# Negated blocks, the addition of value halves, swaps of maxima and a written order in a hybrid attention block

## The chip, the cores and the metric

The kernel runs on one core of one Trainium2 chip. The core has five engines that run their own instructions in order and wait for each other through semaphores: TensorE (PE, matrix products; PEld is its weight load), VectorE (DVE), ScalarE (ACT), GpSimd (POOL) and SyncE (SP, which here only issues transfers). ACT and POOL issue transfers too. The metric is the device time of one execution in microseconds, as the median of three runs. Lower is better.

## The reference

One decoder block in float32 on 1024 tokens, with 16 learned meta tokens ahead of them, a width of 1024 and 8 heads of 64. What matters of it:

```python
h = rmsnorm(x, norm_g)
u_pool, z_pool, q, k, v, z_attn, f, g_pool, g_attn = split(h @ w_in)
y_pool = causal_multiscale_pool(u_pool, pool_w, pool_scale) * silu(z_pool)
log_f = log_sigmoid(f + b_forget)
s = q @ k.T / sqrt(64) + c_query - c_key        # c = cumsum(log_f), causal
y_attn = (softmax(s) @ v) * silu(z_attn)        # per head
merged = sigmoid(g_pool) * (y_pool @ w_up_pool) + sigmoid(g_attn) * (y_attn @ w_up_attn)
out = rmsnorm(x + merged @ w_out, final_norm_g)  # the meta rows are dropped
```

## The kernel before

A float32 product is made of three products of a rounded type: each operand is split into a high and a low part, and hi·hi, hi·lo and lo·hi are summed in PSUM. So an operand always passes a split before PE can use it: the high part is a rounding copy (ACT), the low part a subtraction (POOL for weights, DVE or POOL for activations).

**Stages.** From 0 to about 88 us the input is normalised, transposed into `hh4` and `hl4` (high and low part of the activations, which stay in SBUF) and the queries, keys and values of the first pair of heads are made. From 88 to 520 us run the 16 `Unit`s of the attention: four pairs of heads, two heads each, two halves of the queries each. A unit of the first half has five blocks of keys, one of the second half nine. From 520 to 620 us PE makes the projections `z_pool` and `z_attn` with seven block products where a plain scheme has eight (`g_prod`, 0 to 6, L932), for which sums of blocks of the weights (`GS`) and of the activations (`HS`) are needed. Then come the pooling products, the up projections and the gates (to 707 us), and the output product in seven block products again, with sums of blocks of `w_out` (`TD`).

**The order in the attention.** PE's order is written out by hand. For each unit the scores of the next one (`a_steps`) and the softmax and value products of this one (`c_steps`) are merged, and between them the object `F` ("fill") draws in matmuls of the projections (L164): as many as PACE times the DVE time of a step leaves free, and fixed amounts, LM1 and LM2 (in ns of PE), around `maxes`. The other engines' order is made by a scheduler from the dependencies, and `after(x, y)` adds one by hand.

**Weights.** `split_w` (L141 to L152) loads 128 columns of the weights into a buffer with the tag `raw` (two buffers, SP, L145), and makes the high part on ACT (L150) and the low part on POOL (L152).

**Sums of blocks.** They are made in DRAM during the attention. `put` (L579) is a transfer that SP issues, `add` (L582) one that POOL issues and that adds to its target. The table `SUMS` says which of them follow which unit. `put_neg` (L590) makes the negative of a block of activations: it loads half of the block from DRAM into a tile `neg` with the tag `raw`, ACT negates it (L594) and SP stores it (L595). The tag is that of the weights, so `neg` takes turns with them in the same two buffers.

**Maxima.** `maxes` (L675) takes the running maximum of a unit's scores, transposes it (L678), reduces it (L680), and needs the maximum over four groups of 32 partitions, for which two small copies swap the halves (L682) and four swap the quarters (L685), with a `max` after each (L683, L686). All is on DVE.

**The end of a unit.** `finish` (L721): the value product `po` holds two halves that must be added. ACT copies 64 rows to the tile `t` (L725), DVE adds the others (L726), SP stores the sum to `sp_y` (L727). The row sums `acc` (made on POOL, L707 to L710) are transposed and reduced on DVE (L729, L731) and stored (L732).

**Behind the attention** the scheduler sets the order of ACT, DVE and POOL too. There `w_in_` and `h_in` load blocks of weights and activations, `w_split` (L912) and `h_split` (L921, L922 for product 2, whose activations are negated, and L924, L925 for the others) split them, `keep` (L941), `silu` (L944) and `plus_` (L947) take products out of PSUM, `pool_chain` (L862, L868) makes the moving sums of the pooling branch, `sums_in` (L884 to L889) the reciprocals of the row sums, and `attn_norm` (L841, L842) loads and applies these.

## Time and profile before

| | before |
|---|---|
| runs | 793.66, 793.96, 795.17 us |
| median | 793.96 us |
| the profiled execution's own time | 793.09 us |
| its span | 791.4 us |
| mean granted clock of TensorE | 0.968 |

The profile is one execution; its span runs from the first instruction to the last, and 1.7 us lie around it. In the windows view, each stage's busy time (us; its length; then busy us of each engine with the number of instructions; the granted clock of TensorE as a share of full speed; the busy share of the DMA engines, which can pass 1 where transfers queue; GB/s) reads:

```profile
0.00:88.00 88.00, 85.36 (x570) 74.71 (x571) 46.78 (x117) 49.92 (x110) 28.64 (x50) 1.00 0.32 95
520.00:620.40 100.40, 92.86 (x391) 74.97 (x390) 60.80 (x57) 51.05 (x68) 64.13 (x59) 0.95 0.61 195
707.50:791.40 83.90, 76.35 (x349) 63.52 (x347) 60.23 (x90) 40.71 (x88) 30.02 (x49) 0.98 0.25 89
```

A stage is full where PE's busy time is near its length. Names such as `pj`, `whi` or `neg` are those of the program's tiles; `a<-b` is an instruction that writes a and reads b; x16 is a count; `SPq L145` is the issue of a transfer, and `DMA` the transfer itself. Several figures with slashes are the shortest, median and longest duration.

### The profile page before, as it was taken

To read this page: it belongs to the slowest core of one execution; us is meant where nothing else is said; L and a number is where in the kernel's file an instruction comes from. 1 tells how busy PE (TensorE), PEld (TensorE's weight loads), DVE (VectorE), ACT (ScalarE), POOL (GpSimd) and SP (SyncE) were. 2 spreads that over 40 slices of the span, in tenths; PEclk is the share of its full clock that TensorE was granted. 3 is DMA by queue.
4 is the path that set the end of the run, shared out by engine and by line. 5 is a ranking of instruction groups with operands and counts; after the bars stand their busy time and mean duration, and the time that the engine had idled before them with its cause. 6 is when DMAs were issued, how large, how long until landed. Compare 5 with 4: busy or idle time off the path is not lost.

```text
span 791.4 us, 10759 instructions
## 1 busy us (share of the span) xinstructions
PE 730.7 (92%) x3637; PEld 620.7 (78%) x3637; DVE 554.0 (70%) x1023; ACT 398.3 (50%) x814; POOL 340.2 (43%) x404
## 2 busy tenths in 40 slices
...
PEclk9999999999599979999999999999799999999999
...
GB/s 299 41 28 46 45 83 192 253 33 184 263 35 15 212 263 98 231 91 180 198 64 212 216 179 187 62 276 315 216 147 16 224 107 234 257 241 133 0 1 213
DMA packets 91241, 120.44 MB, mean 152 GB/s; under 512 B 11041, under 2 KB 54049, under 8 KB 91058
## 3 DMA queue, kind: packets, MB, share of 16 engines
...
## 4 chain that ended last, share of the span: by engine, by line
PE 68%; DMA 9%; DVE 8%; ACT 5%; issue 3%; POOL 1%; SPq 0%; POOLq 0%; DVEq 0%; ACTq 0%
PE pj L164 41%; PE pj L1148 8%; PE pj L932 7%; PE po L718 3%; DMA raw<-in_w_in_dram 3%; PE pt L932 2%; PE pt L1148 2%; DMA hsn<-neg 2%; PE ps L657 2%; PE ps L658 2%; ACT S L666 1%; DVE pl L702 1%; DVE m L673 1%; DMA rc<-recs 1%; DMA sp_u<-st 1%
## 5 line engine op out<-in xcount | busy, mean ns | idle before, releaser
L164 PE MATMUL pj<-hh,whi 128*128 128x512 f32 (+3 forms) x640 | 149.1, 360 | 31.8 <-ACT whi L150 28.7
L164 PEld LDWEIGHTS pj<-hh,whi 128*128 128x128 f32 x640 | 110.2, 192 | 45.2 <-ACT whi L150 29.6
L164 PE MATMUL pj<-hl,whi 128*128 128x512 f32 (+3 forms) x640 | 145.5, 354 | 0.0
L152 POOL TENSOR_TENSOR wlo<-raw,whi 128x256 fp32r<-128x256 f32 x116 | 92.7, 886 | 119.3 <-ACT whi L150 61.7
L164 PE MATMUL pj<-hh,wlo 128*128 128x512 f32 (+3 forms) x640 | 143.0, 350 | 0.0
L164 PEld LDWEIGHTS pj<-hl,whi 128*128 128x128 f32 x640 | 109.8, 191 | 12.1
L164 PEld LDWEIGHTS pj<-hh,wlo 128*128 128x128 f32 x640 | 108.4, 188 | 11.9
L702 DVE TENSOR_TENSOR pl<-S,ph 128x512 fp32r<-128x512 f32 (+4 forms) x112 | 88.6, 806 | 15.5 <-ACT ph L701 14.9
L710 POOL TENSOR_TENSOR acc<-acc,S 128x272 f32<-128x272 f32 (+4 forms) x80 | 76.1, 952 | 13.6 <-ACT S L698 8.9
L666 ACT ACTIVATE S<-ps,negc 128x400 f32<-128x400 f32 (+2 forms) x96 | 49.1, 517 | 57.4 <-DVE S L664 54.9
L136 POOL TENSOR_TENSOR gw<-graw,gw 128x256 fp32r<-128x256 f32 x48 | 50.6, 1089 | 39.6 <-ACT gw L912 17.2
L673 DVE TENSOR_TENSOR m<-m,S 128x272 f32<-128x272 f32 (+4 forms) x80 | 48.0, 601 | 26.8 <-ACT S L666 25.3
L698 ACT ACTIVATE S<-S 128x512 f32<-128x512 f32 (+4 forms) x112 | 49.7, 479 | 31.4 <-DVE S L697 31.2
L150 ACT ACTIVATE whi<-raw 128x512 fp32r<-128x512 f32 x58 | 34.2, 623 | 41.0 <-DMA raw<-in_w_in_dram 28.9
L701 ACT ACTIVATE ph<-S 128x512 fp32r<-128x512 f32 (+4 forms) x112 | 51.9, 479 | 1.8 <-PE po L718 1.4
L932 PE MATMUL pj<-gh,gw 128*128 128x512 f32 x180 | 45.8, 411 | 7.5 <-ACT gh L921 6.1
L697 DVE TENSOR_TENSOR S<-S,pt 128x512 f32<-128x512 f32 (+4 forms) x112 | 51.5, 496 | 0.8
L932 PEld LDWEIGHTS pj<-gh,gw 128*128 128x128 f32 x180 | 35.6, 200 | 16.8 <-ACT gh L921 7.3
L657 PE MATMUL ps<-qa,ka 128*128 128x512 f32 (+4 forms) x112 | 38.8, 347 | 7.8 <-ACT S L666 7.3
L1040 DVE TENSOR_TENSOR rl<-pj,rl 128x512 f32<-128x512 f32 x32 | 22.1, 689 | 31.3 <-PE pj L164 31.3
L718 PE MATMUL po<-pl,V 128*128 128x512 f32 (+4 forms) x112 | 38.7, 345 | 3.6 <-DVE pl L702 3.4
L658 PE MATMUL ps<-ql,ka 128*128 128x512 f32 (+4 forms) x112 | 38.3, 342 | 0.0
...
## 6 DMA issues: line engine op xcount, KB each, us to landing
raw<-in_w_in_dram SPq DMA_DIRECT2D x31, 512.0 KB, 6.2
xt<-in_x_dram SPq DMA_DIRECT2D x8, 512.0 KB, 6.7
...
```

The source lines that it names most:

```text
L152: ins = nc.gpsimd.tensor_tensor(lo[:, k:k + 2], raw[:, k:k + 2], r32(hi[:, k:k + 2]), op=ALU.subtract)
L164: nc.tensor.matmul(ps, a, b, start=(i == 0), stop=(i == len(seq) - 1))
L657: nc.tensor.matmul(ps[:kb, c0:], ka[:, k0:k0 + kb], qa[:, q0 + c0:q0 + 512], start=True, stop=False)
L658: nc.tensor.matmul(ps[:kb, c0:], ka[:, k0:k0 + kb], ql[:, q0 + c0:q0 + 512], start=False, stop=True)
L666: nc.scalar.activation(s[:kb, f0:], ps[:kb, f0:], AF.Identity, bias=nb_)
L673: nc.vector.tensor_tensor(m[:kb, c0:], m[:kb, c0:], s[:kb, c0:], op=ALU.max)
L701: nc.scalar.activation(ph[:kb, c0:], s[:kb, c0:], AF.Copy)
L702: dves.append(nc.vector.tensor_tensor(pl[:kb, c0:], s[:kb, c0:], r32(ph[:kb, c0:]), op=ALU.subtract))
L710: accs.append(nc.gpsimd.tensor_tensor(acc[:kb, c0:], acc[:kb, c0:], s[:kb, c0:], op=ALU.add))
L718: nc.tensor.matmul(self.po[:, c0:], v, r[:kb, c0:], start=(b == 0 and i == 0), stop=(b == self.nb - 1 and i == 1))
L932: nc.tensor.matmul(ps, op_w[n][p][k // 2][:, k % 2, i * 128:(i + 1) * 128], op_h[n][q][k // 2][:, k % 2], start=start and m == 0, stop=m = ...
L1148: nc.tensor.matmul(ps, pick(A_, k, p)[:, i * 128:(i + 1) * 128], pick(B_, k, q)[:, c0:c1], start=start and n == 0, stop=n == 11, skip_grou ...
```

## The change

It has four parts.

1. *Negated blocks.* `put_neg` takes 128 rows at a time. It has a buffer of its own (`neg`, 128 x 512), is fed by the split activations that are in SBUF (ACT writes −hi, POOL subtracts the low part in two pieces of 256 columns) and stores the result straight to the places of the sums that need it (`HS` X and A, or C). The blocks 12, 21, n12 and n21 in DRAM are gone, the table of sums is written anew, with 14 adding transfers in place of 16, and the first copies of `TD` 1 and 3 stand next to each other behind unit 4.
2. *The end of a unit.* ACT copies all of `po` to `t`, SP stores one half, and an adding transfer of POOL brings the other half to the same place. DVE's addition is gone.
3. *Maxima.* The six small copies of `maxes` are on ACT.
4. *Order.* PACE goes from 1.74 to 1.67, LM2 from 2600 to 3200. Behind the attention the order of PE, ACT, DVE and POOL is written by hand: `h_split` makes both high parts first, the loads and sums stand earlier, and `attn_norm` later. `pool_chain` is a generator, so that it can be taken in steps. A few tiles have other buffers (`grow`, the weights of product 2), and a low part of the pooling branch moved from POOL to DVE.

```diff
@@ -31,10 +31,10 @@
-PACE = 1.74
+PACE = 1.67
-LM1, LM2 = 1400.0, 2600.0
+LM1, LM2 = 1400.0, 3200.0
...
@@ -397,7 +397,7 @@
-    grow = ap_.tile([1, D], F32, name="grow", tag="t")
+    grow = gp.tile([1, D], F32, name="grow", tag="g")
...
@@ -564,7 +564,7 @@
-    HS = {n: dr.tile([512, 512], F32, name=f"hs{n}") for n in ("11", "12", "21", "22", "n12", "n21", "A", "B", "C", "X")}
+    HS = {n: dr.tile([512, 512], F32, name=f"hs{n}") for n in ("11", "12", "21", "22", "A", "B", "C", "X")}
...
@@ -587,29 +587,41 @@
     def add_h(n):
         add(rows_of(HS[n]), hblock(hl4, n))
 
-    def put_neg(n):
-        for k in range(2):
-            t = wp.tile([128, 2, 512], F32, name="neg", tag="raw")
-            put(t, rows_of(HS[n])[:, 2 * k:2 * k + 2])
-            after(nc.scalar.activation(t, t, AF.Copy, scale=-1.0), exps[-1])
-            nc.sync.dma_start(rows_of(HS["n" + n])[:, 2 * k:2 * k + 2], t)
+    def put_neg(blk, k, *dsts):
+        t = ap_.tile([128, 512], F32, name="neg")
+        after(nc.scalar.activation(t, hblock(hh4, blk)[:, k], AF.Copy, scale=-1.0), exps[-1])
+        for c in range(0, 512, 256):
+            sub = nc.gpsimd.tensor_tensor(t[:, c:c + 256], t[:, c:c + 256], hblock(hl4, blk)[:, k, c:c + 256],
+                                          op=ALU.subtract)
+            after(sub, accs[-1])
+        for d in dsts:
+            put(HS[d][128 * k:128 * k + 128], t)
+
+    def n21(k):
+        put_neg("21", k, "X", "A")
+
+    def n12(k):
+        put_neg("12", k, "C")
+
+    def add_s(d, n):
+        add(rows_of(HS[d]), rows_of(HS[n]))
 
     SUMS = {
-        0: [(put_h, "21"), (put_h, "12")],
-        1: [(add_h, "21"), (put, GS[1], GB["11"])],
-        2: [(add_h, "12"), (put, GS[3], GB["12"])],
-        3: [(put_neg, "21"), (add, GS[1], GB["12"])],
-        4: [(put, TD[1], WB["11"]), (put, TD[3], WB["12"]), (add, GS[3], GB["22"])],
-        5: [(put_neg, "12"), (put_h, "11")],
-        6: [(add, TD[1], WB["12"]), (add_h, "11"), (put, GS[2], GS[3])],
-        7: [(add, TD[3], WB["22"]), (put_h, "22"), (put, HS["X"], HS["n21"])],
-        8: [(add_h, "22"), (add, rows_of(HS["X"]), rows_of(HS["11"]))],
-        9: [(put, TD[2], TD[3]), (put, HS["A"], HS["22"]), (add, GS[2], GB["11"])],
-        10: [(add, TD[2], WB["11"]), (add, rows_of(HS["A"]), rows_of(HS["n21"]))],
-        11: [(put, HS["B"], HS["A"]), (put, GS[4], GS[2])],
-        12: [(put, TD[4], TD[2]), (add, rows_of(HS["B"]), rows_of(HS["11"])), (add, GS[4], GB["21"])],
-        13: [(add, TD[4], WB["21"]), (put, HS["C"], HS["B"])],
-        14: [(add, rows_of(HS["C"]), rows_of(HS["n12"]))],
+        0: [(n21, 0), (put_h, "11")],
+        1: [(n21, 1), (add_h, "11"), (put, GS[1], GB["11"])],
+        2: [(n21, 2), (put_h, "22")],
+        3: [(n21, 3), (add_h, "22"), (add, GS[1], GB["12"])],
+        4: [(add_s, "X", "11"), (put, TD[1], WB["11"]), (put, TD[3], WB["12"])],
+        5: [(n12, 0), (add_s, "A", "22"), (put, GS[3], GB["12"])],
+        6: [(n12, 1), (add, TD[1], WB["12"]), (put, HS["B"], HS["A"])],
+        7: [(n12, 2), (add, TD[3], WB["22"]), (add_s, "B", "11")],
+        8: [(n12, 3), (add, GS[3], GB["22"])],
+        9: [(put, TD[2], TD[3]), (add_s, "C", "B")],
+        10: [(add, TD[2], WB["11"]), (put, GS[2], GS[3])],
+        11: [(add, GS[2], GB["11"])],
+        12: [(put, TD[4], TD[2]), (put, GS[4], GS[2])],
+        13: [(add, TD[4], WB["21"])],
+        14: [(add, GS[4], GB["21"])],
     }
 
     def sums_of(i):
@@ -679,10 +691,10 @@
             r, x, r2, y, mx = [sm.tile([128, 16], F32, name=n) for n in ("mr", "mx", "ms", "my", "mz")]
             nc.vector.tensor_reduce(r, mt.rearrange("p (j b) -> p j b", b=32), axis=AX.X, op=ALU.max)
             for a, b in ((0, 64), (64, 0)):
-                nc.vector.tensor_copy(x[a:a + 64], r[b:b + 64])
+                nc.scalar.activation(x[a:a + 64], r[b:b + 64], AF.Copy)
             nc.vector.tensor_tensor(r2, r, x, op=ALU.max)
             for a, b in ((0, 32), (32, 0), (64, 96), (96, 64)):
-                nc.vector.tensor_copy(y[a:a + 32], r2[b:b + 32])
+                nc.scalar.activation(y[a:a + 32], r2[b:b + 32], AF.Copy)
             nc.vector.tensor_tensor(mx, r2, y, op=ALU.max)
             self.pm = psT.tile([128, 512], F32, name="pt")
             nc.vector.transpose(self.pm, mx[:, :, None].to_broadcast([128, 16, 32]))
@@ -722,9 +734,10 @@
             hr, lr = rows(self.e)
             po, acc = self.po, self.acc
             t = ap_.tile([128, 512], F32, name="t")
-            nc.scalar.activation(t[hr], po[lr], AF.Copy)
-            nc.vector.tensor_tensor(t[hr], po[hr], t[hr], op=ALU.add)
-            nc.sync.dma_start(spill["y", self.p][hr, self.q0:self.q0 + 512], t[hr])
+            nc.scalar.activation(t, po, AF.Copy)
+            yd = spill["y", self.p][hr, self.q0:self.q0 + 512]
+            nc.sync.dma_start(yd, t[hr])
+            after(nc.gpsimd.dma_start(yd, t[lr], accum_op=ALU.add), accs[-1])
             at = ap_.tile([KB, 512], F32, name="mt")
             after(nc.vector.transpose(at, acc), dves[-1])
             r = sm.tile([128, 16], F32, name="sr")
...
@@ -900,30 +915,31 @@
             nc.sync.dma_start(tiles[k], rows_of(src)[:, 2 * k:2 * k + 2])
 
     def w_in_(n):
-        pool, tag = (hq, "w") if n in (4, 6) else (wp, "raw")
+        pool, tag = {2: (gp, "g"), 4: (0, "w"), 6: (0, "w")}.get(n, (wp, "raw"))
+        pool = pool or hq
         g_load(raw_w, n, GSRC[n], [pool.tile([128, 2, 512], F32, name="graw", tag=tag) for _ in range(2)])
 
     def h_in(n):
         g_load(raw_h, n, HSRC[n], [wp.tile([128, 2, 512], F32, name="hraw", tag=t) for t in ("wh", "wl")])
 
-    def w_split(n):
-        hi, lo = [[bp.tile([128, 2, 512], F32R, name="gw", tag="y", bufs=8) for _ in range(2)] for _ in range(2)]
+    def w_split(n, k):
+        if not k:
+            op_w[n] = [[bp.tile([128, 2, 512], F32R, name="gw", tag="y", bufs=8) for _ in range(2)] for _ in range(2)]
+        hi, lo = op_w[n]
+        nc.scalar.activation(hi[k], raw_w[n][k], AF.Copy)
+        for c in range(2):
+            pool_tt(lo[k][:, c], raw_w[n][k][:, c], r32(hi[k][:, c]), ALU.subtract)
+
+    def h_split(n):
+        op_h[n] = [[hq.tile([128, 2, 512], F32R, name="gh", tag="h") for _ in range(2)] for _ in range(2)]
+        hi, lo = op_h[n]
         for k in range(2):
-            nc.scalar.activation(hi[k], raw_w[n][k], AF.Copy)
-            for c in range(2):
-                pool_tt(lo[k][:, c], raw_w[n][k][:, c], r32(hi[k][:, c]), ALU.subtract)
-        op_w[n] = hi, lo
-
-    def h_split(n, neg=False):
-        hi, lo = [[hq.tile([128, 2, 512], F32R, name="gh", tag="h") for _ in range(2)] for _ in range(2)]
+            nc.scalar.activation(hi[k], raw_h[n][k], AF.Copy, scale=-1.0 if n == 2 else 1.0)
         for k in range(2):
-            if neg:
-                nc.scalar.activation(hi[k], raw_h[n][k], AF.Copy, scale=-1.0)
+            if n == 2:
                 nc.vector.scalar_tensor_tensor(lo[k], raw_h[n][k], -1.0, r32(hi[k]), op0=ALU.mult, op1=ALU.subtract)
             else:
-                nc.scalar.activation(hi[k], raw_h[n][k], AF.Copy)
                 nc.vector.tensor_tensor(lo[k], raw_h[n][k], r32(hi[k]), op=ALU.subtract)
-        op_h[n] = hi, lo
...
@@ -943,70 +959,104 @@
     def silu(z, ps, scale=1.0):
         evacs.append(nc.scalar.activation(z, ps, AF.Silu, scale=scale))
 
-    def plus_(dst, ps, scale):
+    def plus_(dst, ps):
         nc.vector.tensor_tensor(dst, ps, dst, op=ALU.add)
-        silu(dst, dst, scale)
-
-    pool_chain(3)
-    pool_chain(2)
+
+    def prods(ps, n, start, order=range(4)):
+        for i in order:
+            g_prod(ps[i], n, i, start)
+
+    for i in range(4):
+        za[i], zp[i] = btile("za"), btile("zp")
+    cg = {g: pool_chain(g) for g in range(4)}
     w_in_(1)
-    for p in range(3):
-        attn_in(p)
-    w_split(1)
+    next(cg[3])
     h_in(2)
     w_in_(2)
-    for i in range(4):
-        g_prod(ga_[i], 0, i, True)
-        za[i] = btile("za")
-        keep(za[i][:, T0_], ga_[i])
+    for k in range(2):
+        w_split(1, k)
+    run(cg[3])
+    M2 = ExitStack()
+    M2.enter_context(tc.manual_schedule(engines={mybir.EngineType.PE, mybir.EngineType.Activation,
+                                                 mybir.EngineType.DVE, mybir.EngineType.Pool}))
+    prods(ga_, 0, True)
+    h_in(3)
+    keep(za[0][:, T0_], ga_[0])
+    w_split(2, 0)
+    keep(za[1][:, T0_], ga_[1])
+    w_split(2, 1)
+    keep(za[2][:, T0_], ga_[2])
+    keep(za[3][:, T0_], ga_[3])
+    w_in_(3)
     sums_in()
-    pool_chain(1)
-    w_split(2)
-    for i in range(4):
-        g_prod(gb_[i], 1, i, True)
-        plus_(za[i][:, T0_], gb_[i], 1.0)
+    prods(gb_, 1, True)
     HX.close()
     hq = ctx.enter_context(tc.tile_pool(name="hq", bufs=8, side="right", reuse_waits="tile"))
-    h_split(2, True)
-    h_in(3)
-    w_in_(3)
-    w_split(3)
+    h_split(2)
+    next(cg[2])
+    next(cg[2])
+    plus_(za[0][:, T0_], gb_[0])
+    next(cg[2])
+    plus_(za[1][:, T0_], gb_[1])
+    run(cg[2])
+    plus_(za[2][:, T0_], gb_[2])
+    attn_in(0)
+    attn_in(1)
+
+    prods(ga_, 2, False)
     h_split(3)
+    for k in range(2):
+        w_split(3, k)
+    plus_(za[3][:, T0_], gb_[3])
+    w_in_(4)
+    h_in(4)
+    run(cg[1])
     for i in range(4):
-        g_prod(ga_[i], 2, i, False)
-        zp[i] = btile("zp")
         keep(zp[i][:, T0_], ga_[i])
-    pool_chain(0)
+    attn_norm(0)
+    attn_in(2)
+
+    prods(gb_, 3, True)
...```

Lines of the changed kernel that the orders below name: L579 and L582 are `put` and `add` as before, L592 and L594 the negation on ACT and POOL, L694 and L697 the small copies, L714 the low part of the softmax, L719 to L722 the row sums `acc`, L737, L739 and L740 the copy, the store and the adding transfer of `finish`, L742 to L745 the transposed row sums, L855 `y` of `attn_norm`, L875 and L882 the moving sums, L899 to L904 `sums_in`, L940 and L942 the low parts of `h_split`, L963 `plus_`.

**SP's queue behind units 3 and 4.** The names are `raw` for weights, `sp_y` for a unit's result, `sp_gp` for results of the fill, `hsn` and `hsX`, `hsA` for negated blocks and sums, `td` for the sums of `w_out`. Before:

```order
L727 DMA sp_y_768<-t 64x512
L579 DMA neg<-hs_782 128x2x512
L884 DMA fin<-sums 32x16x16
L595 DMA hsn_785<-neg 128x2x512
L337 DMA sp_gp_2204<-st 128x512
L595 DMA hsn_785<-neg 128x2x512
L145 DMA raw<-in_w_in_dram 128x8x128
L579 DMA td_772<-in_w_out_dram 512x512
L145 DMA raw<-in_w_in_dram 128x8x128
L579 DMA td_774<-in_w_out_dram 512x512
L145 DMA raw<-in_w_in_dram 128x8x128 x2
```

Now:

```order
L739 DMA sp_y_768<-t 64x512
L579 DMA hsX<-neg 128x512
L579 DMA hsA<-neg 128x512
L899 DMA fin<-sums 32x16x16
L337 DMA sp_gp_2209<-st 128x512
L579 DMA td_772<-in_w_out_dram 512x512
L579 DMA td_774<-in_w_out_dram 512x512
L145 DMA raw<-in_w_in_dram 128x8x128
L745 DMA sums<-sr 128x16
L145 DMA raw<-in_w_in_dram 128x8x128
L739 DMA sp_y_769<-t 64x512
```

The loads of `neg` are gone, its stores go to `hsX` and `hsA` and no load of `raw` uses their buffer; the two copies to `td` moved together, ahead of the next load of weights.

**POOL around units 5 and 6.** Before, the row sums of one unit and the next table entry:

```order
L710 TENSOR_TENSOR acc<-acc,S 128x144
L710 TENSOR_TENSOR acc<-acc,S 128x16
L707 COPY acc<-S 128x112
L708 TENSOR_TENSOR acc<-S 128x400
L710 TENSOR_TENSOR acc<-acc,S 128x272
L710 TENSOR_TENSOR acc<-acc,S 128x144
L710 TENSOR_TENSOR acc<-acc,S 128x16
L582 DMA td_772<-in_w_out_dram 512x512
L582 DMA hs_780<-hl_120 128x4x512
```

Now:

```order
L582 DMA hsA<-hs_783 128x4x512
L594 TENSOR_TENSOR neg<-neg,hl_122 128x256 x2
L719 COPY acc<-S 128x112
L720 TENSOR_TENSOR acc<-S 128x400
L722 TENSOR_TENSOR acc<-acc,S 128x272
L740 DMA sp_y_769<-t 64x512
L722 TENSOR_TENSOR acc<-acc,S 128x144
L722 TENSOR_TENSOR acc<-acc,S 128x16
L582 DMA td_772<-in_w_out_dram 512x512
```

The subtractions of `neg` and the adding transfer of the last unit's result (`sp_y`) now stand among the row sums of the next unit.

**DVE behind the attention.** Before, the low parts of products 2 and 3 (`gh`) among the sums of product 1 (`za`) and the normalisations (`y`):

```order
L947 TENSOR_TENSOR za<-pj,za 128x512 x2
L842 TENSOR_TENSOR y<-y,rc 128x1024
L947 TENSOR_TENSOR za<-pt,za 128x512
L922 SCALAR_TENSOR_TENSOR gh<-hraw,gh 128x1024
L842 TENSOR_TENSOR y<-y,rc 128x1024
L922 SCALAR_TENSOR_TENSOR gh<-hraw,gh 128x1024
L925 TENSOR_TENSOR gh<-hraw,gh 128x1024 x2
```

Now:

```order
L904 STREAM_TRANSPOSE fin<-fin 128x64
L940 SCALAR_TENSOR_TENSOR gh<-hraw,gh 128x1024 x2
L875 TENSOR_TENSOR s_5718<-u 128x1039
L875 TENSOR_TENSOR s_5719<-s_5718 128x1037
L963 TENSOR_TENSOR za<-pj,za 128x512
L875 TENSOR_TENSOR s_5718<-s_5719 128x1033
L963 TENSOR_TENSOR za<-pj,za 128x512
L882 SCALAR_TENSOR_TENSOR u<-s_5718,u 128x1024
L963 TENSOR_TENSOR za<-pj,za 128x512
L942 TENSOR_TENSOR gh<-hraw,gh 128x1024 x2
```

The low parts of product 2 (L940) moved ahead of the sums of product 1 and of all normalisations; the first of these (L855) now stands behind the low parts of product 3 (L942).

75 lines of the change are left out of this document (45 added, 30 removed).

## The prediction

> **What bounds the kernel now.** I read the page's shares first, then the waits of the tensor engine, then the chain of waits inside the longest of them.
>
> ```profile
> span 791.4 us, 10759 instructions
> PE 730.7 (92%) x3637; PEld 620.7 (78%) x3637; DVE 554.0 (70%) x1023; ACT 398.3 (50%) x814; POOL 340.2 (43%) x404
> PEclk9999999999599979999999999999799999999999
> ```
>
> PE is busy for 92% of the span. All that the change can win without taking matmuls away is the other 60.7 us (791.4 − 730.7) and what the low digits of the granted clock cost. The number of matmuls stays the same. The table of waits (engine and operation, what released it; us in total, times, longest) says which idle time matters:
>
> ```profile
> PE pj L164 <- ACT whi L150: 28.7, 2, 17.2
> PE ps L657 <- ACT S L666: 7.3, 8, 2.6
> PE pj L932 <- ACT gh L921: 6.1, 2, 5.7
> PE po L718 <- DVE pl L702: 3.4, 6, 1.0
> PE pj L164 <- DVE V L304: 3.0, 2, 2.8
> PE pj L932 <- DVE gh L922: 1.4, 1, 1.4
> ```
>
> Two waits make 28.7 us: a projection's matmul (L164) waits for the high part of its weights. The chain of waits through both (start us, us, what) shows why these come late:
>
> ```profile
> 192.88 0.95 ACT neg L594
> 193.86 3.46 DMA hsn<-neg
> 197.38 11.14 DMA raw<-in_w_in_dram
> 208.55 0.64 ACT whi L150
> 261.94 4.71 DMA neg<-hs
> 266.68 1.07 ACT neg L594
> 267.76 9.74 DMA hsn<-neg
> 277.57 8.70 DMA raw<-in_w_in_dram
> ```
>
> The weights' buffer `raw` is lent to `neg`. A block is loaded, negated and stored, and only when the store has landed may the next weights be loaded. The four stretches below are the two stalls and the half-speed time behind each (us; length; busy us of PE, PEld, DVE, ACT, POOL; granted clock, DMA share, GB/s):
>
> ```profile
> 192.07:209.23 17.16, 0.00 (x0) 0.00 (x0) 1.71 (x3) 3.98 (x8) 2.67 (x4) 0.58 1.02 256
> 209.23:215.40 6.17, 6.17 (x15) 4.82 (x16) 0.91 (x1) 2.78 (x5) 4.84 (x7) 0.50 1.05 311
> 275.40:286.97 11.57, 0.00 (x0) 0.00 (x0) 6.05 (x16) 0.68 (x2) 0.00 (x0) 0.71 1.12 269
> 286.97:290.50 3.53, 3.53 (x12) 3.53 (x13) 0.00 (x0) 2.10 (x4) 3.49 (x6) 0.51 1.18 392
> ```
>
> A third loss lies where block product 2 waits for its activations (first the chain, then the stretch, then a dense stretch for scale):
>
> ```profile
> 556.17 1.75 DVE y L842
> 557.92 1.68 DVE gh L922
> ...
> 548.81:563.50 14.69, 7.15 (x15) 4.74 (x16) 12.40 (x10) 8.14 (x10) 10.81 (x8) 0.65 0.65 187
> 620.40:707.50 87.10, 87.10 (x386) 71.97 (x385) 53.74 (x80) 33.06 (x46) 7.72 (x10) 1.00 0.62 215
> ```
>
> DVE does a normalisation of the attention (`y`, L842) between the two parts of `gh` that PE wants.
>
> **The change part by part.** The sum starts at the profiled execution's own 793.1 us (span 791.4 and 1.7 around it). The median shown is 794.0, 0.9 above and inside the runs' own spread (793.66 to 795.17).
>
> *Negated blocks in SBUF: −28.7 and −4.8.* `neg` has its own buffer and is made from the split activations, so no weight load waits for a store of `neg` any more. The 17.16 and 11.57 us go. Behind them the clock stood at 0.50 for 6.17 us and at 0.51 for 3.53 us: 6.17 × 0.50 + 3.53 × 0.49 = 4.8 us of lost speed that has no stall to follow. What is late next is the weight load again, if something else on SP's queue holds it; that is a rival below. The added work is eight quarters: each one ACT copy (0.62 us, as `whi` below), two POOL subtractions and one or two stores.
>
> ```profile
> L150 ACT ACTIVATE whi<-raw 128x512 fp32r<-128x512 f32 x58 | 34.2, 623 | 41.0 <-DMA raw<-in_w_in_dram 28.9 <-PE pj L164 11.2 <-issue 0.8
> L152 POOL TENSOR_TENSOR wlo<-raw,whi x116: 717/742/1788, 47.9 to 511.2; 128x256 fp32r<-128x256 f32 x116
> 88.00:520.00 432.00, 389.06 (x1948) 335.58 (x1947) 332.49 (x682) 223.52 (x505) 209.74 (x237) 0.96 0.61 154
> ```
>
> On ACT that is 8 × 0.62 = 5 us in place of four of about 1.0 (the rows of `neg` in the chain above). On POOL it is 16 × 0.74 = 12 us more, in a stage of 432 us where POOL is busy for 210. The cover is ample and I count nothing, but the subtractions delay what stands behind them; that is in the term of new waits. Two large POOL transfers and the copies between DRAM tensors go too. Their gain in DMA traffic I put at nothing, since no wait of PE but those above ends in a DMA.
>
> *The order behind the attention: −9.7.* In 14.69 us PE does 15 matmuls that take 87.10 / 386 = 0.226 us each in the dense stretch, so 3.4 us of work and 11.3 us of loss. After the change both high parts of `gh` come first on ACT, both low parts stand on DVE ahead of the normalisation, and the 1.75 us of `y` are out of their way. What remains: the second pair of buffers is free only behind product 1's last matmul, then one high part (about 1.0, as `neg` has the same size) and one low part (1.7) must follow, 2.7 us, of which five matmuls on the first half cover 5 × 0.226 = 1.1. I keep 1.6 as loss: 11.3 − 1.6 = 9.7. Bounds: nothing gained if another operand (the weights of product 2) is late instead, 11.3 if all is hidden.
>
> *Copies of the maxima on ACT, the addition off DVE: −4.* Per unit (16 of them) DVE loses the addition and six small copies; ACT's copy of the product grows from 64 to 128 rows at the same length.
>
> ```profile
> L726 DVE TENSOR_TENSOR t<-po,t x16: 662/688/696, 114.7 to 515.4; 64x512 f32<-64x512 f32 x16
> L682 DVE COPY mx<-mr x32: 167/170/614, 91.4 to 490.7; 64x16 f32<-64x16 f32 x32
> L666 ACT ACTIVATE S<-ps,negc 128x16 f32<-128x16 f32 x16 | 4.3, 272 | 10.8 <-DVE S L664 10.8
> ```
>
> DVE is relieved of 0.69 + 6 × 0.17 = 1.7 us a unit, 27 us of its 332 in this stage. The path of the maxima itself gets longer where nothing lies beside it: six copies take 6 × 0.27 = 1.6 us by the nearest ACT row with sixteen columns, for 1.0 now. In their time DVE can transpose and reduce the row sums (`mt<-acc`, 0.71 us, and a reduction), which now stand between its copies. PE's waits that hang on DVE sum to 7.3 + 3.4 + 3.0 = 13.7, so the bounds are −14 and, with 0.6 us more on the path in every unit, +10. I take −4: only the 7.3 us have the maxima ahead of them, and half of these.
>
> [...]
>
> *The halves added by a transfer: +6.* SP stores one half, POOL issues a transfer that adds the other, and its issue waits in order until the first has landed.
>
> ```profile
> DMA to landing us min/median/max: 2.2/2.3/6.0
> L582 POOL DMA_DIRECT2D td<-in_w_out_dram x4: 1022/1024/1071, 263.7 to 454.1; - x4
> 254.96 0.71 DVE L729 STREAM_TRANSPOSE mt<-acc 128x512 f32<-128x512 f32 x1
> 250.46 1.06 POOL L710 TENSOR_TENSOR acc<-acc,S 128x144 f32<-128x144 f32 x2
> ```
>
> The first row is that of the store of `t` (`sp_y`, L727). It now lands 2.3 us after its issue, and a POOL issue of a larger transfer takes 1.0. So POOL stands some 3 us in each unit. Behind it are queued the additions to `acc`, for which DVE's transpose `mt<-acc` waits, and the splits `wlo` of the next weights. In unit 5, shown above, `acc` was ready at 251.5 and DVE came to it at 255.0: 3.4 us of slack, just enough. In the last unit the additions ended at 508.1 and the transpose began at 508.8:
>
> ```profile
> 503.02 5.10 POOL L710 TENSOR_TENSOR acc<-acc,S 128x512 f32<-128x512 f32 x5
> 508.83 0.70 DVE L729 STREAM_TRANSPOSE mt<-acc 128x512 f32<-128x512 f32 x1
> ```
>
> Bounds: nothing where slack covers all, and 16 × 1 us where each unit loses the issue alone. I take +6, six tight units of the sixteen, with SP's new waits for POOL's subtractions among their causes. The new values of PACE and LM2 only shift which filling matmuls are drawn where; their sum is the same, and I count nothing, within the bounds just given.
>
> *The end of the attention: +1.* The split of product 1's second weights lies in the space of `t` and must wait until the last adding transfer has landed. ACT stands at it, and behind it is the evacuation for which product 0's third bank waits. The landing may cost 0 to 5 us (2.3 + 2.3 + 1.0 with no slack); product 0's first banks cover most.
>
> **Sum:** 793.1 − 28.7 − 4.8 − 9.7 − 4 + 6 + 1 = 752.9, so 753 us.
>
> **The rivals.** *POOL in lock step (765 to 778).* Half the units lose 1.5 to 3 us because POOL waits for SP's store: 8 × 1.5 = 12 up to 8 × 3 = 24 on top. For it: three engines in order now wait for each other in each unit. Against it: POOL is idle for 222 of 432 us. The Trainium skill, "SBUF — State Buffer", section "SBUF: two separate sides", adds that descriptors of POOL's transfers cannot be written while DVE runs certain copies. The rows of L582 here keep within 1.02 to 1.07 us for one kind, which shows no such stall; at half a microsecond a unit it would be 8 us, 761.
>
> *The stalls move (785 to 794).* The weight load is still late, behind other things in SP's order: stores of `neg` that wait for POOL, and two copies between weights and DRAM that now follow each other directly. One such copy took 5.07 us to issue already:
>
> ```profile
> 198.47 5.07 SPq L579 DMA_DIRECT2D td<-in_w_out_dram  x1
> ```
>
> Then the change does not do what it says; with 28.7 + 4.8 back the time is 786. Against it: by the order of the changed program a buffer of weights comes free about three column blocks of 48 matmuls ahead of its use, 3 × 48 × 0.226 = 32 us, and a load takes 9 to 11 of them even in the stalls above. One stall of two would give 753 + 17.2 or 753 + 11.6, so 765 to 770.
>
> *Slower (over 795).* POOL's in-order wait grows with the landing of the store. The stores of `neg` show how far that can go:
>
> ```profile
> hsn<-neg SPq DMA_DIRECT2D x4, 512.0 KB, 9.7
> ```
>
> If `sp_y` landed after 9.7 us instead of 2.3 in each unit, POOL would stand 7.4 us longer each time, `acc` would be late by that, and a slack like unit 5's would cover 3.4 of it. 4 us a unit reach PE: 753 + 16 × 4 = 817. It decides from (793 − 753) / 16 = 2.5 us a unit, so from a landing of 8.2 us. Against it: `sp_y` has never taken more than 6.0.
>
> **How the numbers follow.** Forecast, 743 to 763: 0.62. Lock step or one stall left, 763 to 778: 0.17. Better than 743 (all of DVE's 14 us and no new waits give 736): 0.06. The stalls move, 785 to 796 (the upper end with the products' 9.7 not gained either): 0.07, of which 0.04 within 0.2%. Slower: 0.08. A run of this kernel can tell about 0.2% (1.6 us) from no change. So faster 0.88, same 0.04, slower 0.08. With every bound at its low end the sum is 753 − 10 − 6 − 1 − 1.6 = 734, with every one at its high end 753 + 14 + 10 + 4 + 9.7 = 791. They will not all fall one way; two thirds of each distance give 740 and 778, which leaves out the last two cases and little of the others.
>
> **What would show it.** The wait of L164's matmul for `whi` falls from 28.7 to under 3 us, and the granted clock has no slice at 5 or 7 before the products. The first matmul of product 2 follows product 1's last within some 3 us. The wait of `ps` for `S` is half of 7.3 or less. POOL's wait for `sp_y` shows at the accumulating transfer, about 2 us each, and DVE's transposes of `acc` do not wait for POOL in more than six units. The prediction is wrong if PE still shows a gap over 5 us ahead of 500 us, or if `mt<-acc` waits for POOL in most units.

## The result and the profile after

| | before | after |
|---|---|---|
| median of 4 runs | 793.81 us | 771.82 us |
| range | 793.0 to 795.17 | 769.52 to 773.84 |
| the profiled execution's own time | 793.09 us | 771.57 us |
| its span | 791.4 us | 769.8 us |
| mean granted clock | 0.968 | 0.982 |

The ratio of the times is 0.972, with a 95% interval from 0.969 to 0.9751. The kernel is 22 us faster. The prediction was 753, with a range from 740 to 778: right in direction and range, but 19 us too low, and outside the 743 to 763 of its likeliest case.

The page's shares, and the waits of TensorE (what waited, for what; us in total, times, longest), of the changed kernel:

```profile
PE 727.8 (95%) x3637; PEld 619.5 (80%) x3637; DVE 538.6 (70%) x913; ACT 416.9 (54%) x914; POOL 352.4 (46%) x430
PEclk9999999998999999999999999999997999999999
...
PE pj L948 <- DVE zp L963: 10.0, 1, 10.0
PE ps L669 <- ACT S L678: 9.9, 14, 2.1
PE po L730 <- DVE pl L714: 6.8, 3, 3.8
...
PE pj L164 <- DVE V L304: 0.4, 1, 0.4
```

The wait of L164 for `whi`, 28.7 us, is gone. A new one stands at the top: a block product (L948) waits 10.0 us for DVE. The waits that hang on DVE in the attention (`S`, `pl`, `V`) sum to 17.1 us, where they were 13.7; that of the scores for `S` alone went from 7.3 to 9.9.

Which stretch gained, by the windows view? The bounds are the last value product's end, the first and the last block product of z, and the start of the output product. First the attention before, then the rows of the changed kernel:

```profile
88.00:513.25 425.25, 382.31 (x1919) 330.00 (x1918) 328.43 (x678) 222.33 (x503) 209.74 (x237) 0.96 0.61 153
526.60:620.42 93.82, 86.28 (x362) 69.55 (x361) 55.16 (x50) 48.58 (x66) 62.50 (x58) 0.95 0.59 185
```

```profile
88.00:486.00 398.00, 380.53 (x1925) 330.46 (x1925) 316.56 (x567) 241.48 (x605) 232.29 (x266) 0.98 0.62 147
498.66:599.37 100.71, 85.83 (x362) 68.17 (x361) 55.96 (x56) 47.35 (x63) 52.66 (x53) 0.95 0.51 167
```

The attention ends 27.25 us earlier (425.25 − 398.00). The block products behind it take 6.9 us more (100.71 − 93.82). The stretch between the two is 0.7 us shorter, and all that follows takes 0.5 us less: −27.25 − 0.7 + 6.9 − 0.5 = −21.6, the difference of the spans.

The place of the 10 us, in the changed kernel's windows and its DVE timeline (start us, us, engine, line, operation; in brackets the idle time before and what ended it):

```profile
572.56:582.57 10.01, 0.00 (x1) 0.03 (x1) 5.97 (x8) 5.08 (x10) 1.01 (x2) 0.64 0.19 53
582.57:590.00 7.43, 7.43 (x26) 6.01 (x27) 2.62 (x4) 3.24 (x6) 3.63 (x6) 0.80 0.39 106
...
576.90 1.22 DVE L855 TENSOR_TENSOR y<-y,rc 128x1024 f32<-128x1024 f32 x1 [2.24 <-DMA rc<-recs]
578.04 0.68 DVE L963 TENSOR_TENSOR zp<-pt,zp 128x512 f32<-128x512 f32 x1
578.64 1.28 DVE L963 TENSOR_TENSOR zp<-pj,zp 128x512 f32<-128x512 f32 x2
581.13 0.69 DVE L1069 TENSOR_TENSOR wlu<-rawu,whu 128x512 fp32r<-128x512 f32 x1 [1.21 <-ACT whu L1068]
581.74 0.68 DVE L963 TENSOR_TENSOR zp<-pj,zp 128x512 f32<-128x512 f32 x1
```

PE had ended product 5 and the first pooling product at 572.56. The sums `zp` that free the PSUM banks for product 6 needed nothing more, but in DVE's written order the last normalisation (L855) stands ahead of them and waits for its load `rc`; ahead of the last sum stands `wlu`, which waits for ACT. The lower clock behind the gap (0.80 in the mean of 7.43 us) costs 7.43 × 0.20 = 1.5 us more.

### The profile page after: what moved, and what is told of

The parts are those of the page before. It is cut to its first block, busy times and chain, and to the rows that moved or that the text cites. A ratio compares the mean times of both kernels' runs of the same rounds, so it can differ in the third digit from the quotient of the medians.

```text
span 769.8 us, 10843 instructions
## 1 busy us (share of the span) xinstructions
PE 727.8 (95%) x3637; PEld 619.5 (80%) x3637; DVE 538.6 (70%) x913; ACT 416.9 (54%) x914; POOL 352.4 (46%) x430
## 4 chain that ended last, share of the span: by engine, by line
PE 60%; DVE 16%; ACT 8%; issue 6%; DMA 3%; POOL 1%; POOLq 0%; SPq 0%; DVEq 0%; ACTq 0%
PE pj L164 35%; PE pj L1203 8%; PE pj L948 6%; DVE pl L714 4%; DVE S L709 2%; PE po L730 2%; PE pt L1203 2%; PE pt L948 2%; ACT S L678 2%; ACT S L710 2%; DVE m L685 1%; PE ps L669 1%; PE ps L670 1%; DMA hraw<-hs 1%; ACT ph L713 1%
## 5 line engine op out<-in xcount | busy, mean ns | idle before, releaser
L164 PE MATMUL pj<-hh,whi 128*128 128x512 f32 (+3 forms) x640 | 146.4, 356 | 0.4 <-DVE V L304 0.4
L164 PE MATMUL pj<-hl,whi 128*128 128x512 f32 (+3 forms) x640 | 145.1, 356 | 0.0
L164 PE MATMUL pj<-hh,wlo 128*128 128x512 f32 (+3 forms) x640 | 144.1, 352 | 0.0
L152 POOL TENSOR_TENSOR wlo<-raw,whi 128x256 fp32r<-128x256 f32 x116 | 94.9, 941 | 97.5 <-ACT whi L150 48.0
L164 PEld LDWEIGHTS pj<-hl,whi 128*128 128x128 f32 x640 | 110.7, 193 | 12.5
L164 PEld LDWEIGHTS pj<-hh,whi 128*128 128x128 f32 x640 | 109.5, 191 | 12.4 <-PE pj L294 0.6
L164 PEld LDWEIGHTS pj<-hh,wlo 128*128 128x128 f32 x640 | 108.9, 190 | 11.7
L714 DVE TENSOR_TENSOR pl<-S,ph 128x512 fp32r<-128x512 f32 (+4 forms) x112 | 98.1, 888 | 22.4 <-ACT ph L713 21.5
L722 POOL TENSOR_TENSOR acc<-acc,S 128x272 f32<-128x272 f32 (+4 forms) x80 | 77.7, 971 | 8.4 <-ACT S L710 2.8
L678 ACT ACTIVATE S<-ps,negc 128x400 f32<-128x400 f32 (+2 forms) x96 | 48.5, 514 | 57.4 <-DVE S L676 52.6
L685 DVE TENSOR_TENSOR m<-m,S 128x272 f32<-128x272 f32 (+4 forms) x80 | 52.4, 655 | 23.2 <-ACT S L678 21.1
L136 POOL TENSOR_TENSOR gw<-graw,gw 128x256 fp32r<-128x256 f32 x48 | 48.5, 1065 | 28.9 <-ACT gw L929 28.9
L710 ACT ACTIVATE S<-S 128x512 f32<-128x512 f32 (+4 forms) x112 | 49.2, 478 | 19.6 <-DVE S L709 19.5
L948 PE MATMUL pj<-gh,gw 128*128 128x512 f32 x180 | 45.0, 403 | 13.8 <-DVE zp L963 10.0
L948 PEld LDWEIGHTS pj<-gh,gw 128*128 128x128 f32 x180 | 34.4, 194 | 23.4 <-issue 10.4
L669 PE MATMUL ps<-qa,ka 128*128 128x512 f32 (+4 forms) x112 | 38.0, 340 | 9.9 <-ACT S L678 9.9
L730 PE MATMUL po<-pl,V 128*128 128x512 f32 (+4 forms) x112 | 38.6, 345 | 7.4 <-DVE pl L714 6.8
L720 POOL TENSOR_TENSOR acc<-S 128x400 f32<-128x400 f32 (+1 forms) x16 | 20.2, 1266 | 39.0 <-ACT S L710 39.0
```

Of the source, the lines that this page charges most:

```text
L152: ins = nc.gpsimd.tensor_tensor(lo[:, k:k + 2], raw[:, k:k + 2], r32(hi[:, k:k + 2]), op=ALU.subtract)
L164: nc.tensor.matmul(ps, a, b, start=(i == 0), stop=(i == len(seq) - 1))
L678: nc.scalar.activation(s[:kb, f0:], ps[:kb, f0:], AF.Identity, bias=nb_)
L685: nc.vector.tensor_tensor(m[:kb, c0:], m[:kb, c0:], s[:kb, c0:], op=ALU.max)
L710: exps.append(nc.scalar.activation(s[:kb, c0:], s[:kb, c0:], AF.Exp))
L714: dves.append(nc.vector.tensor_tensor(pl[:kb, c0:], s[:kb, c0:], r32(ph[:kb, c0:]), op=ALU.subtract))
```

## The experiments

All times are medians of four or more executions beside the kernel before on the same chip (793.6 to 794.8 there), each with its ratio to that kernel and the 95% interval in brackets; `m1_lock` ran once.

**The written order, undone or mended.** `e4_old_tail` keeps everything of the attention and puts back the code of before behind it, buffers and the low part of the pooling branch included.

```diff
-    M2 = ExitStack()
-    M2.enter_context(tc.manual_schedule(engines={mybir.EngineType.PE, mybir.EngineType.Activation,
-                                                 mybir.EngineType.DVE, mybir.EngineType.Pool}))
-    prods(ga_, 0, True)
...
+    pool_chain(3)
+    pool_chain(2)
+    w_in_(1)
...
```

> The changed kernel in everything up to the end of the attention, with the work behind it in the order of the kernel before (scheduler, loads late). Theory, from the two traces: first to last block product takes 100.7 us in the changed kernel and 93.8 before, so the written order loses 7 us: 771.6 - 7 = 765 (761 to 769). Rival, the prediction's own step: the written order wins 9.7 us, so without it 781.

Measured: 761.58 us, ratio 0.9599 [0.9566, 0.9632]. The windows of its block products:

```profile
496.25:587.15 90.90, 86.69 (x362) 69.85 (x361) 60.42 (x55) 48.65 (x66) 59.54 (x54) 0.94 0.58 182
```

90.9 us in place of 100.7. The written order loses some 10 us by the times; the rival, that it wins, is refuted. The size is less sure than the sign. From the last value product to the end of the span the changed kernel takes 283.8 us, and nine traces with the order of before take 274.1 (this one, the shortest) to 278.5: 5 to 10 us. Product 2's wait for `gh`, 5.7 us at its longest before, is 2.5 here and 6.0 in `e6_add_dve`, with the same code behind the attention.

`e1_norm_last` moves one thing in it:

```diff
-    attn_norm(3)
     for i in (3, 2, 1):
         plus_(zp[i][:, T1_], ga_[i])
...
     silu(zp[0][:, T1_], zp[0][:, T1_], -1.0)
+    attn_norm(3)
```

> The changed kernel with the last normalisation of the attention (attn_norm(3), its two loads and its DVE product) moved behind DVE's sums of product 5. Theory: DVE stands at this normalisation for a load (rc) while the sums that free PE's banks for product 6 are queued behind it; that is the 10.0 us gap ahead of product 6, with some 1.5 us of half-speed clock after it. Without it 771.6 - 11 = 760 us (757 to 763), the wait of product 6 for zp under 2 us. Rival: the low part of the up weights (wlu), which also stands ahead of the last sum on DVE and waits for ACT, takes its place: a gap of 3 to 5 us stays, 764 to 767. Second rival: the gap is not DVE's order but the late release of a buffer, and comes back at another place: 770.

Measured: 768.96 us, 0.968 [0.9655, 0.9705], about 3 us by the ratios, not 11, and with overlapping intervals. The gap ahead of product 6 halved:

```profile
PE pj L948 <- DVE zp L963: 5.1, 1, 5.1
...
577.49 0.69 DVE L1068 TENSOR_TENSOR wlu<-rawu,whu 128x512 fp32r<-128x512 f32 x1 [1.22 <-ACT whu L1067]
578.10 0.68 DVE L963 TENSOR_TENSOR zp<-pj,zp 128x512 f32<-128x512 f32 x1
```

The rest is the first rival's mechanism, though not its time (764 to 767): `wlu` stands ahead of the last sum and waits for ACT. A wait in product 5 for `gh` also grew, from 0.7 to 2.2 us. So I moved three things in the changed kernel:

```diff
-    attn_norm(2)
 
     prods(ga_, 5, False, (3, 2, 1, 0))
...
-    attn_norm(3)
+    attn_norm(2)
     for i in (3, 2, 1):
         plus_(zp[i][:, T1_], ga_[i])
         silu(zp[i][:, T1_], zp[i][:, T1_], -1.0)
...
-    ws[0, 0] = up_weights(0, 0)
     plus_(zp[0][:, T1_], ga_[0])
     silu(zp[0][:, T1_], zp[0][:, T1_], -1.0)
+    ws[0, 0] = up_weights(0, 0)
+    attn_norm(3)
```

> The changed kernel with three places of the written order of DVE changed: the last normalisation behind the sums of product 5 (as e1_norm_last), the last of these sums ahead of the low part of the up weights instead of behind it, and the normalisation of the third pair behind the low parts of product 6. Theory: what e1_norm_last kept (a wait of 5.1 us of product 6 and 2.3 us of product 5, with half clock behind) is of the same kind, DVE instructions that wait for a load or for ACT ahead of one that PE wants: 769.0 - 8 = 761 (758 to 764). Rival: the loads of rc or the splits of the last weights are late by themselves, and the wait comes back in product 5 or 6: 767 or more.

Measured: 770.09 us, 0.9695 [0.9668, 0.9722], no better than `e1_norm_last`; product 6 waited 8.3 us. The DVE timeline, and the chain of waits at the same place, say why:

```profile
577.26 1.23 DVE L855 TENSOR_TENSOR y<-y,rc 128x1024 f32<-128x1024 f32 x1 [3.76 <-DMA rc<-recs]
578.41 0.68 DVE L963 TENSOR_TENSOR zp<-pt,zp 128x512 f32<-128x512 f32 x1
...
571.37 1.39 PE pj L164 x6
572.76 0.24 SPq L854
573.05 4.12 DMA rc<-recs
```

I had put the third pair's normalisation where the fourth's had stood, ahead of the sums, and it waited in the same way. SP can issue the load of `rc` only when the pooling products (L164) have ended, by the chain at 572.76. So the load is late by itself, as the rival had it, and a normalisation at this place, the third pair's or the fourth's, makes DVE wait. A written order with both behind the sums was not tried.

`e9_best` adds the halves on DVE in this kernel.

> As e8_norms_late, with the halves of the value product added on DVE (as e6_add_dve, which gained 3.8 us). Theory: both gains add, 761 - 4 = 757 (753 to 760), the fastest so far or level with e6_add_dve (757.8). Rival: the adding transfer's cost depends on the order behind the attention, and nothing is gained here: 761.

Measured: 765.81 us, 0.9634 [0.9606, 0.9662]: 4 us faster than `e8_norms_late`, as expected, but from the higher start. It is not the fastest.

**The stalls: the buffer or SP's order.** `e2_own_buffer` gives `neg` one buffer of its own in the kernel before, and still makes it through DRAM, in quarters of 128 rows spread over units 3 to 6 and 8 to 11.

```diff
-    def put_neg(n):
-        for k in range(2):
-            t = wp.tile([128, 2, 512], F32, name="neg", tag="raw")
-            put(t, rows_of(HS[n])[:, 2 * k:2 * k + 2])
+    def put_neg(n, k):
+        t = ap_.tile([128, 512], F32, name="neg")
+        put(t, rows_of(HS[n])[:, k])
...
```

> The kernel before, with one thing changed: neg has a buffer of its own (quarters of 128 rows, spread over units 3 to 6 and 8 to 11), but is loaded from DRAM and stored to DRAM as before. Theory: the two stalls came from the shared buffer alone, so 28.7 and some 4 us of half clock go: 793.8 - 33 = 761 (757 to 767). Rival: SP's order was the cause, as its stores of neg wait in front of the weight loads; these waits are still there, and one or both stalls return in a new place: 775 or more.

Measured: 787.18 us, 0.993 [0.9902, 0.9959]. Of 33 us only 6 came. TensorE's waits for `S`, and the chain of waits in one of the two long ones (8.8 us; the other is 9.8):

```profile
PE ps L656 <- ACT S L665: 27.5, 13, 9.8
...
197.38 12.83 DMA neg<-hs
210.55 0.04 ACT neg L593
211.09 0.58 ACT S L665
211.72 0.60 PE ps L656
```

No weight is late now, but the same wait has changed its engine: the negation stands in ACT's queue, waits 12.8 us for its load, and the scores' activation `S` stands behind it. The rival's time holds, but not its mechanism, which looked at SP's order. One own buffer alone doesn't do it. In the longer wait it is itself part of the cause: the load stands behind the store of the quarter before (6.9 us) and then takes 8.0. Two own buffers were not tried; with the block in SBUF already, as in the next run, both waits are gone.

**What making it in SBUF is worth by itself.** `e3_neg_only` is the kernel before with the new `put_neg`, `SUMS` and the buffer of `grow`.

```diff
+        t = ap_.tile([128, 512], F32, name="neg")
+        after(nc.scalar.activation(t, hblock(hh4, blk)[:, k], AF.Copy, scale=-1.0), exps[-1])
+        for c in range(0, 512, 256):
+            sub = nc.gpsimd.tensor_tensor(t[:, c:c + 256], t[:, c:c + 256], hblock(hl4, blk)[:, k, c:c + 256],
...
```

> The kernel before with one part of the change: negated blocks made in SBUF with their own buffer, and the new table of sums. Maxima, addition of halves, PACE, LM2 and the order behind the attention are as before. Theory: this part carries the whole gain of the attention, 794 - 33.5 = 761 (757 to 766), and no wait of L164 for whi over 2 us is left. Rival: the loads of weights are still late behind SP's stores and the two td copies, and one stall of 11 to 17 us stays: 770 or more.

Measured: 775.57 us, 0.9768 [0.974, 0.9796]: 18 us, not 33. Yet no weight is late any more. The windows of its attention and of one new wait with the half-speed stretch behind it, and what DVE and POOL did there:

```profile
88.00:496.50 408.50, 385.25 (x1921) 332.08 (x1920) 344.66 (x678) 222.04 (x508) 221.03 (x251) 0.97 0.56 139
182.66:186.97 4.31, 0.00 (x2) 0.00 (x1) 4.31 (x3) 0.00 (x0) 3.81 (x5) 0.93 1.07 185
186.97:193.00 6.03, 6.03 (x18) 5.06 (x18) 4.74 (x15) 2.70 (x10) 0.00 (x0) 0.50 1.12 209
...
180.37 5.54 DVE L683 TENSOR_TENSOR m<-S 128x400 f32<-128x400 f32 x1 [0.55 <-ACT S L678]
...
180.42 1.92 POOL L594 TENSOR_TENSOR neg<-neg,hl 128x256 f32<-128x256 f32 x2
181.80 1.58 POOL L582 DMA_DIRECT2D gs<-in_w_in_dram  x1
182.51 3.96 POOL L152 TENSOR_TENSOR wlo<-raw,whi 128x256 fp32r<-128x256 f32 x4
```

PE's idle time in the attention is 23.3 us (408.5 − 385.25), against 42.9 before; without the 28.7 of the two stalls it would be 14.2. So 9 us of new waits came, with half-speed clock behind them: PE's busy time rose by 2.9 us instead of falling by 4.8. DVE's own work did not change, yet its 678 instructions took 344.7 us here and 328.4 before. The last rows point to the cause. An operation of DVE that reads two tiles of SBUF took 5.54 us (its median is 0.83), and as long POOL ran subtractions, with one issue among them, without a pause. The changed kernel has the same at the same place, with 5.97 us at a clock of 0.50 behind it:

```profile
181.07 5.04 DVE L685 TENSOR_TENSOR m<-m,S 128x272 f32<-128x272 f32 x1 [0.45 <-ACT S L678]
183.19:187.03 3.84, 0.00 (x0) 0.00 (x1) 3.84 (x3) 0.00 (x0) 3.48 (x5) 0.89 1.07 203
```

**That cost by itself.** `m1_lock` computes nothing of the reference. POOL makes one subtraction, then n more; DVE makes one operation behind the first.

```python
nc.gpsimd.tensor_tensor(w[0], g, b[:, :256], op=ALU.subtract)
if dma:
    nc.gpsimd.dma_start(land.pop(), land2, accum_op=ALU.add)
for i in range(n):
    nc.gpsimd.tensor_tensor(w[1 + i % 7], a[:, 256:512], b[:, 256:512], op=ALU.subtract)
nc.vector.tensor_tensor(z, w[0], f[:, :256], op=ALU.subtract)     # ss;  ps reads PSUM in place of f
```

> A measurement by itself; nothing of the reference is computed. POOL makes one subtraction of 128x256, then n more without a pause (n = 0, 1, 2, 4, 7), in half of the cases with the issue of a small adding transfer between; DVE makes one operation of 128x256 behind the first subtraction, either with two inputs in SBUF (ss) or with one in SBUF and one in PSUM (ps). Theory: a DVE operation with two SBUF inputs stands while POOL runs and can stand through several of POOL's operations, so ss grows from about 0.3 us with n to several us, ps does not. Rival: only the issue of a transfer by POOL blocks DVE: ss and ps grow with the issue by about 1 us and not with n. Second rival: the long DVE operations of the traces have another cause, and nothing grows.

The view of DVE's two lines (count: shortest, median, longest in ns; the digits are n, the d marks the issue of a transfer, and names without digits hold all n together):

```profile
L96 DVE TENSOR_TENSOR ss<-w,f x20: 425/929/4975, 7.7 to 198.9; 128x256 f32<-128x256 f32 x20
L96 DVE TENSOR_TENSOR ss0d<-w,f x4: 424/424/426, 12.8 to 37.3; 128x256 f32<-128x256 f32 x4
L96 DVE TENSOR_TENSOR ss2d<-w,f x4: 426/515/2426, 88.7 to 97.6; 128x256 f32<-128x256 f32 x4
L96 DVE TENSOR_TENSOR ss7d<-w,f x4: 425/529/5793, 204.7 to 223.7; 128x256 f32<-128x256 f32 x4
L98 DVE TENSOR_TENSOR ps<-ps,w x20: 423/424/426, 38.8 to 246.1; 128x256 f32<-128x256 f32 x20
L98 DVE TENSOR_TENSOR ps7d<-ps,w x4: 424/424/425, 251.5 to 270.1; 128x256 f32<-128x256 f32 x4
```

With one input in PSUM the operation always takes 0.42 us. With both in SBUF it takes 0.42 us where no subtraction follows, and up to 5.0 us without and 5.8 us with an issue where seven follow. The issue alone (`ss0d`) costs nothing. The theory holds: the operation can stand while POOL makes several subtractions.

When it does so is not settled. Without an issue it took 0.93 us where it began 0.07 us behind the first subtraction, and 1.6 to 5.0 us where it began 0.5 us or more behind. With an issue and n of 1 or more, DVE's operation begins ahead of the subtractions by the records in all 16 cases, by 0.03 to 0.48 us, and still stood 2.4 to 5.8 us in four of them. So the order of the records alone does not decide it.

The Trainium skill, "SBUF — State Buffer", section "Who interferes with whom", says that such an operation contends with a GpSimd instruction that reads SBUF, and that whoever issues first holds the ports for the whole instruction. The runs agree that the two contend, and go further: DVE stood through several of POOL's instructions, not one, and in four cases although its record begins first.

`e10_neg_dve` takes the 16 subtractions off POOL in `e3_neg_only`:

```diff
-        for c in range(0, 512, 256):
-            sub = nc.gpsimd.tensor_tensor(t[:, c:c + 256], t[:, c:c + 256], hblock(hl4, blk)[:, k, c:c + 256],
-                                          op=ALU.subtract)
-            after(sub, accs[-1])
+        after(nc.vector.tensor_tensor(t, t, hblock(hl4, blk)[:, k], op=ALU.subtract), dves[-1])
```

> As e3_neg_only (775.6), with the low part of the negated blocks subtracted on DVE (one operation of 128x512) and not on POOL. Theory: the new waits of PE in e3_neg_only (2.1, 4.3 and 3.4 us, with half clock behind) follow DVE operations of 4 to 5.5 us that stand behind runs of POOL's subtractions; with 16 of these fewer, runs are shorter: two of the three waits go and 4 to 8 us with them, 768 to 772, and DVE shows fewer operations over 2 us. Rival: the runs of the weights' low parts (wlo) do it alone, or DVE's load counts for more: 775 or slower.

Measured: 768.64 us, 0.9677 [0.9655, 0.9699], 7 us faster, as expected. Windows of its attention:

```profile
88.00:488.10 400.10, 379.79 (x1918) 329.14 (x1918) 336.36 (x686) 223.10 (x507) 211.25 (x235) 0.98 0.57 142
```

PE's idle time there is 20.3 us against 23.3, and its busy time 379.8 against 385.3. DVE's busy time fell from 344.7 to 336.4, with eight operations more. The wait of 4.3 us was gone and that of 2.1 halved, while one of 2.4 us came elsewhere. Of the 15 us that `e3_neg_only` fell short of its forecast gain, 7 are the subtractions; the other 8 were not shown apart.

**The other parts, each taken out of `e4_old_tail`.** The maxima back on DVE:

```diff
-                nc.scalar.activation(x[a:a + 64], r[b:b + 64], AF.Copy)
+                nc.vector.tensor_copy(x[a:a + 64], r[b:b + 64])
...
```

> As e4_old_tail (761.6), with the six small copies of the maxima back on DVE. Theory: the prediction's term, of which half or more is from the maxima: 2 to 4 us slower, 764 to 766, with more wait of ps for S. Rival: the copies' place does not matter, as ACT's path is no shorter: 760 to 763. Third: ACT's copies are the longer path (page's price, some 0.6 us a unit): 5 us faster, 757.

Measured: 772.38 us, 0.9725 [0.9691, 0.9758], 10 to 11 us slower, more than any of the three cases expected. In the traces the attention takes 404.8 us in place of 395.6, 9.2 more: 5.2 of PE's idle time and 4.0 of its busy time, at a granted clock of 0.98 in place of 0.99. The traced executions differ by 13.6 us; the other 4.4 lie behind the attention, where the code is the same. The timeline of a unit's maxima in `e4_old_tail` (DVE, then ACT), and of another of the same kind in `e5_maxima_dve`:

```profile
410.56 0.69 DVE L692 TENSOR_REDUCE mr<-mt 128x16 f32<-128x512 f32 x1
411.35 0.71 DVE L742 STREAM_TRANSPOSE mt<-acc 128x512 f32<-128x512 f32 x1
412.10 0.69 DVE L744 TENSOR_REDUCE sr<-mt 128x16 f32<-128x512 f32 x1
413.29 0.73 DVE L700 STREAM_TRANSPOSE pt<-mz 128x512 f32<-128x512 f32 x1
411.28 0.44 ACT L694 ACTIVATE mx<-mr 64x16 f32<-64x16 f32 x2 [2.05 <-DVE mr L692]
412.15 0.89 ACT L697 ACTIVATE my<-ms 32x16 f32<-32x16 f32 x4 [0.43 <-DVE ms L695]
```

```profile
419.29 0.69 DVE L692 TENSOR_REDUCE mr<-mt 128x16 f32<-128x512 f32 x1
422.81 0.73 DVE L700 STREAM_TRANSPOSE pt<-mz 128x512 f32<-128x512 f32 x1
```

From the reduction's end to the transpose it is 2.04 us with ACT's copies (413.29 − 411.25) and 2.83 without (422.81 − 419.98). Worked out in the same way from the rows of all 16 units, the sums are 37.0 and 50.8 us: 13.8 us less of a chain on which the next scores wait. ACT's copies lie beside the row sums, as the prediction had it, and take 0.22 us each (0.89 for four).

The halves added on DVE:

```diff
-            nc.scalar.activation(t, po, AF.Copy)
-            nc.sync.dma_start(yd, t[hr])
-            after(nc.gpsimd.dma_start(yd, t[lr], accum_op=ALU.add), accs[-1])
+            nc.scalar.activation(t[hr], po[lr], AF.Copy)
+            nc.vector.tensor_tensor(t[hr], po[hr], t[hr], op=ALU.add)
...
```

> As e4_old_tail (761.6), with the halves of the value product added on DVE again and no adding transfer. Theory: POOL's in-order wait and issue cost what DVE's addition cost, 760 to 764. Rival: POOL's waits behind the stores (the prediction's +6) are real, and without them it is 5 us or more faster, 756. Third: DVE's relief is the larger part: 765 or more.

Measured: 757.83 us, 0.9548 [0.952, 0.9576], about 4 us faster, although DVE has 16 additions more; in the traces the attention takes 391.4 us in place of 395.6. The intervals of the two overlap a little, but `e9_best` shows the same 4 us. The loss was not where I looked for it. In the changed kernel's table of waits no operation of DVE waits for `acc`, and POOL's own wait for the first half's store is in two units, nearly all of it in one:

```profile
POOL sp_y L740 <- DMA sp_y<-t: 11.8, 2, 11.3
```

What the adding transfer costs is spread over PE's small waits (for `S` 9.3 us in `e4_old_tail` and 7.6 in `e6_add_dve`, for `pl` 6.8 and 4.8). The longest operation of DVE at the place shown above is as long with the adding transfer as without (5.04 and 5.01 us). What makes the small waits was not shown apart.

PACE and LM2 as before:

```diff
-PACE = 1.67
+PACE = 1.74
-LM1, LM2 = 1400.0, 3200.0
+LM1, LM2 = 1400.0, 2600.0
```

> As e4_old_tail (761.6), with PACE 1.74 and LM2 2600 as before. Theory, as the prediction had it: the sum of the fill is the same, 760 to 763. Rival: the new values take waits of ps for S away, so with the old ones 4 us or more are lost, 765 or more.

Measured: 765.23 us, 0.9646 [0.9607, 0.9685], 3.6 us slower, with overlapping intervals: a gain of the new values is likely, but not settled.

**The fastest kernel.** `e11_neg_add_dve` is `e6_add_dve` with the subtractions of `e10_neg_dve`.

> As e6_add_dve (757.8: the change without the written order behind the attention and without the adding transfer), with the low part of the negated blocks subtracted on DVE as in e10_neg_dve. Theory: POOL's runs of subtractions are shorter, fewer DVE operations stand behind them, and 3 to 6 us of PE's waits and half clock go: 752 to 755. Rival: DVE's added 8 operations of 0.7 us cost as much where the maxima are on ACT already: 757 to 759.

Measured: 758.42 us, 0.9535 [0.951, 0.956], level with `e6_add_dve`; the rival holds. So the 7 us of `e10_neg_dve` are not to be had here. The two starting kernels differ in the maxima and in PACE and LM2, and which of these decides was not tried. At the place shown above DVE's operation fell from 5.01 to 2.94 us and PE's wait from 2.8 to 1.7, but a new wait of 3.8 us came later (`ps` for `S`). Both beat the two kernels of this case: the change without its written order and without its adding transfer runs in 758 us.

## Why the prediction was right or wrong

*Its steps, by the terms of its sum.*

- **The stalls (−28.7 and −4.8).** The mechanism was right: the wait for `whi` went entirely. The term was mis-sized. By itself this part gained 18 us and not 33.5. Of the 15 us between, 7 are POOL's added subtractions, which lengthened runs behind which DVE stands (`e10_neg_dve`); the rest stays open. The prediction saw that POOL's idle time covers their 12 us and counted nothing. It looked at whether POOL had time, and not at whom POOL holds up.
- **The order behind the attention (−9.7): this is the step that failed.** Product 2's wait for `gh` did go, from 5.7 us to 1.0 at its longest. The step asked "what is late next" only for product 2's own operands, down to product 2's weights. What was late next stood four products further: a normalisation that waits for its load, and then `wlu`, ahead of the sums for product 6, 10.0 us, and 4.9 us of small waits. The stretch grew by 6.9 us, and with the order of before the kernel is 10 us faster (`e4_old_tail`; 5 to 10 by the traces). Its bounds, from nothing to 11.3 gained, had left a loss out.
- **Maxima and addition (−4).** Mis-sized, and in one term that should have been two. The maxima alone are worth 10 to 11 us by the times, 9.2 by the attention's traces. The prediction feared a path 0.6 us longer in every unit, with six copies at 1.6 us; they took 0.44 + 0.89 = 1.33, the row sums lay beside them, and the path got some 0.8 shorter. It also weighed the term by the waits that PE showed before, and 4.0 of the 9.2 us are PE's busy time, longer at the lower clock.
- **The halves added by a transfer (+6).** About right in size: 4 us by `e6_add_dve`. The place was wrong, as no transpose of `acc` on DVE is seen to wait for POOL. So neither the lock step nor the slower rival came about; the store lands after 3.2 us in the median. The waits of `ps` for `S`, which should have halved, grew.
- **PACE and LM2 (nothing).** Likely some 3 us of gain.
- **The end of the attention (+1).** The stretch to the first block product is 0.7 us shorter.

The attention as a whole came out 27.25 us shorter where the terms say 31.5. The single terms were further off than that, and offset each other: 15 us too much for the stalls, some 7 too little for the maxima, 3 for PACE. That the attention came so near is luck in part. The 19 us are the attention's 4.25 and the written order, 6.9 + 9.7 = 16.6 us, less 1.7 at the end of the attention and 0.5 behind.
